# Down projection of six feed-forward blocks in seven products of quarter blocks, and another estimate of the shared port

## The chip, the cores and the metric

The kernel runs on one core of a Trainium2 chip. The metric is device time in microseconds (us) of one execution; the profile is of one execution of the same program. Engines are named as in the profile: PE (TensorE), PEld (its weight loads), DVE (VectorE), ACT (ScalarE), POOL (GpSimd), SP (the queue that issues the loads).

## The reference, cut to what matters

One layer of a decoder trunk for a prompt group of 512 tokens and a sample group of 8 x 4 tokens, all in float32. After four mixers and a first LayerNorm comes the feed-forward part, to which the change belongs:

```python
D_MODEL = 2048
D_FF = 4 * D_MODEL
...
mix = jnp.concatenate([y_a, y_b, y_c, y_d], axis=-1) @ lp['w_out']
x = layer_norm(ALPHA * x + mix, lp['ln1_g'], lp['ln1_b'])
ff = jnp.square(jax.nn.relu(x @ lp['w_up'])) @ lp['w_down']
x = layer_norm(ALPHA * x + ff, lp['ln2_g'], lp['ln2_b'])
```

## The kernel before

Activations lie transposed: a tile has 128 features on the partitions and 544 tokens (512 prompt, 32 sample) on the free axis, worked in two halves of HN = 272. The profile's names A, B, C, E and F are such slots of one pool; during the feed-forward part the 16 tiles `z` of the residual sum are E and A0 to A14, and the normalised input `x1h`, `x1l` lies in B, C and F.

Every float32 product is made of three matmuls in the rounded type fp32r: a value is split into a rounded part and the rest (`uh` and `ul`, `x1h` and `x1l`, for weights `wh` and `wl`), and `mm3` adds wh x xh, wh x xl and wl x xh. Weights come in parts of 128 x 1024 floats (512 KB) into a ring of `raw` buffers, loaded by SP (`emit_dma`); three of these buffers and four of each split ring exist from the start, and `widen` adds NRAW2 = 2 and NPIECE2 = 1 in the space that the mixers leave. A piece of 512 columns is split by one ACT copy into `wh` (`emit_split`) and one subtraction into `wl` (`emit_lo`), on DVE, or for units planned with None on DVE or POOL, whichever the planner's clocks say. Five pieces are made ahead of TensorE, and the next piece is begun when one has been used up (`piece_done`). A part's buffer is loaded anew after its last subtraction.

The feed-forward part goes over 8 blocks of 1024 hidden features. In each block 8 up tiles (16 k tiles x 2 halves x 3 = 96 matmuls of 272 columns each) are made, squared after relu and split (`up_done`); the first block's are made half by half as 16 units of 48 matmuls (`uph`). Then 16 down tiles (8 k tiles x 2 halves x 3 = 48 matmuls each) are added into `z` by DVE. Two down tiles share a unit of weights 256 columns wide. The last block's down tiles are made in two passes, with the second LayerNorm (`finish`) beside them. The first pass over `w_out` before the feed-forward part ends with units (`op`, `ob`) in which each accumulator takes a chain of 12 matmuls, 4 k tiles x 3, on one half.

The order of all instructions is fixed when the program is built, by a planner (`Model`): it keeps a clock for each engine, a price for each instruction, and for instructions of DVE and POOL the stretches in which they hold a port that the two share. Side work (`gens`) is put between matmuls when it is due by these clocks, and POOL or DVE is chosen by them. `in_sbuf` decides which inputs count as lying in SBUF. Tile names carry two numbers (such as acc_57_205), so that cutting off the last number leaves acc_57, which is not in the list ("s", "t", "o", "acc") of accumulators.

Every instruction is recorded at line 159, the planner's wrapper, so rows are told apart by tile names.

Of the kernel before, what the change touches and what calls it, by code (L numbers as in the profile page):

```python
# [33 lines left out]
NT = NP + NS  # L34
# [13 lines left out]
LN2_B = -2.12194440054690583e-4  # L48
SCALE = 0.125
NQ = 3  # L50
NRAW2, NPIECE2 = 2, 1
AT2, AT3 = 4.0, 4.0
NSTEP = 1
ZB, ZV = 0.0, 0.3
# [2 lines left out]
LV, LA, LM = 2.5, 2.0, 2.5  # L57
AHEAD = 3
GBIAS = 2.0


TABLES = {str(f) for f in (AF.Exp, AF.Sigmoid, AF.Sin, AF.Gelu_apprx_tanh, AF.Sqrt)}
# [80 lines left out]
class Engine:  # L143
    PER = {"V": (0.00104, 0.155), "A": (0.00083, 0.19), "G": (0.0021, 0.19)}

    @staticmethod
    def in_sbuf(x):

        name = getattr(x, "tensor", x).name
        return name.rsplit("_", 1)[0] not in ("s", "t", "o", "acc") and x.shape[-1] > 1  # L150

    def __init__(self, mdl, eng, name):
        self.mdl, self.eng, self.nme = mdl, eng, name
# [58 lines left out]
def tile_hybrid_trunk(ctx: ExitStack, tc: tile.TileContext, x_prompt, x_sample, cache_nsa_kv, cache_win_kv,  # L212
# [130 lines left out]

    NPIECE, NRAW, PART = 4, 3, 1024
    raws, pieces, parts, plan, split, pending = {}, [], [], [], {}, []
    st = {"piece": 0, "dma": 0}

    def add_unit(src, kc, cols, lo=None):

        i = len(plan)  # L350
        plan.append((kc, cols, lo))
        n = max(1, PART // cols)
        for a in range(0, kc, n):
            parts.append((i, src(a, min(a + n, kc)), min(n, kc - a), cols))
            w = min(n, kc - a) * cols
            for q in range(0, w, 512):
                pieces.append((i, a * cols + q, min(512, w - q), len(parts) - 1, q))
        return i

    def ring(tag, i, shape, dt, n, n2):  # L360

        if "wide" in st and (i - st["wide"][tag]) % (n + n2) < n2:
            return alloc(ffp, tag + "2", shape, dt, n2)
        return alloc(wgt, tag, shape, dt, n)
# [19 lines left out]
    def emit_split():  # L384

        pi = st["piece"]
        if pi >= len(pieces):
            return
        emit_lo()
        u, a, n, part, q = pieces[pi]  # L390
        hi = ring("wh", pi, (128, 512), F32R, NPIECE, NPIECE2)
        A.copy(hi[:, :n], raws[part][:, q:q + n])
        pending.append((pi, hi))
        st["piece"] = pi + 1

    def emit_lo():
        if pending:
            pi, hi = pending.pop()
            u, a, n, part, q = pieces[pi]
            raw = raws[part][:, q:q + n]  # L400
            lo = ring("wl", pi, (128, 512), F32R, NPIECE, NPIECE2)
            eng = plan[u][2]
            if eng is None:
                eng = V if mdl.clk["V"] + 0.65 + GBIAS < mdl.clk["G"] + 1.25 else G
            eng.tensor_sub(lo[:, :n], raw, hi[:, :n])
            split[u, a] = (hi, lo)
            if pi + 1 == len(pieces) or pieces[pi + 1][3] != part:
                if st["dma"] < len(parts):
                    emit_dma()
# [120 lines left out]
    def up_cols(b_, i):  # L530
        return lambda a, b: [(whole, dram2(w_up, a * 128 * DFF + b_ * 1024 + i * 128,
                                           [[DFF, 128], [128 * DFF, b - a], [1, 128]]))]

    def dn_cols(b_, n):
        return lambda a, b: [(whole, dram2(w_down, (b_ * 1024 + a * 128) * DM + n * 128,
                                           [[DM, 128], [128 * DM, b - a], [1, 256]]))]

    for h in range(2):
        for i in range(NA):
# [1 line left out]
    for b in range(NBLK):  # L541
        for i in range(NA if b == 0 else 0, 8):
            U["up", b, i] = add_unit(up_cols(b, i), KT, 128, V)
        for h in range(2 if b == NBLK - 1 else 1):
            for n in range(0, 16, 2):
                U["dn", b, h, n] = add_unit(dn_cols(b, n), 8, 256, None if b == NBLK - 1 else V)
# [1301 lines left out]

    x1h, x1l = mh, ml
    sums = {}  # L1850

    def lnq(h, tag, bufs=1):
        return alloc(S["lnp", h], "ln" + tag, (128, HN), F32, bufs)

    def sum_add(k, h):

        if k == 0:
            if not sums:
                sums["t"] = slot(lo_slots.pop())
            sums[h] = sums["t"][:, hs_(h)]  # L1860
            G.tensor_copy(sums[h], z[k][:, hs_(h)])
        else:
            G.tensor_add(sums[h], sums[h], z[k][:, hs_(h)])

    def norm_stats(ln, h):
# [3 lines left out]
        hold(mean)  # L1869
        mm(mean[:, :HN], ones_f, sums[h])  # L1870
        if "v" not in sums:
            sums["v"] = slot(lo_slots.pop())
        va, vb = sums["v"][:, :HN], sums["v"][:, HN:]
        yield mean,
        q = {}
# [82 lines left out]
    uh, ul = {}, {}  # L1958
    ur = lambda k: (uh[k], ul[k])

    def up_done(i, acc, hv=(0, 1)):
        if 0 in hv:
            uh[i], ul[i] = fq(f"uh{i}", F32R), fq(f"ul{i}", F32R)
        t = fq("sq", bufs=2)
        a, b = hv[0] * HN, hv[-1] * HN + HN
        tv = halves(t)[:, hv[0]:hv[-1] + 1]
        av = acc[:, hv[0]:hv[-1] + 1, :HN]
        A.activation(tv, av, AF.Relu)
        V.tensor_mul(tv, tv, av)
        split_hl(uh[i][:, a:b], ul[i][:, a:b], t[:, a:b])  # L1970

    for h in range(2):
        drain_side(("rstd", 1, h))
# [25 lines left out]
    def finish(h):  # L1999
# [6 lines left out]
        def chunk(c, i):  # L2006
# [10 lines left out]
            yield y,  # L2017
            V.tensor_scalar(nm_[:n, i, c:c + 1], s_[:n, i, c:c + 1], -1.0 / 512, None, op0=OP.mult)
            yield nm_,
            sq = fq("sq", bufs=2)  # L2020
            A.activation(sq[:n, :512], y[:n], AF.Square, bias=nm_[:n, i, c:c + 1], accum_out=m2[:n, i, c:c + 1])
            mdl.put(mdl.ready, m2, mdl.when(sq, read=False))
            flags.add(("st", h, c, i))
# [41 lines left out]
        for c in range(4):  # L2065
            for i in range(ng):
                yield rstd, ("lag", "V", 2.5)
                apply(c, i, nmu, rstd, t_)

    for b in range(NBLK):  # L2070
        for i in range(NA if b == 0 else 0, 8):
            up_done(i, run_tile(U["up", b, i], 0, 128, x1r, ks16, True))
        last = b == NBLK - 1
        if last:
            load_gb()
        for h in range(2 if last else 1):
# [43 lines left out]
```

## Time and profile before

| | |
|---|---|
| median of 3 runs | 2548.75 us (2545.38 to 2549.04) |
| profiled execution: its time, its span | 2549.48 us, 2547.7 us |
| mean granted clock of TensorE | 0.966 |
| busy: PE, PEld, DVE, ACT, POOL | 95%, 91%, 44%, 35%, 23% |
| DMA | 260.80 MB, 102 GB/s |

PE's busy share counts pipelined matmuls and says only that something was under way. What one matmul costs is read from the distance between the starts of neighbours.

### The profile page before, as it was taken

How to read it: one execution, taken by the hardware profiler on the slowest of the kernel's cores; microseconds unless marked ns; L12 is line 12 of the kernel's file. 1: busy time of each engine (PE TensorE's matmuls, PEld its weight loads, DVE VectorE, ACT ScalarE, POOL GpSimd, SP SyncE). 2: the span in 40 equal slices, each digit the busy share in tenths (PEclk: the TensorE clock that was granted, in tenths of full speed). 3: DMA queues.
4: the chain of work that ended last, by engine and by line, in shares of the span. 5: the costliest groups of instructions: out<-in, count | busy, mean ns of one | idle time of the engine just before them, and what ended most of it. 6: DMA issues, size and time to landing. Idle time of an engine off the chain costs nothing.

```text
span 2547.7 us, 46688 instructions
## 1 busy us (share of the span) xinstructions
PE 2417.4 (95%) x19283; PEld 2329.7 (91%) x19283; DVE 1112.8 (44%) x2009; ACT 882.5 (35%) x1725; POOL 594.1 (23%) x552
## 2 busy tenths in 40 slices
PE   6999999998998687999999999999999999999995
PEld 6999888988888486999999999999999999999995
DVE  6773344566645656333333333333333333333346
ACT  4443345554444445422222222222222212212353
POOL 2332235446446487400000000000000000000155
PEclk8999999999999787999999999999999999999998
DMA  7333322321386443423223223223223223223343
GB/s 222 72 84 83 117 71 61 88 76 52 94 216 207 116 125 108 141 90 94 83 86 98 84 84 99 84 83 96 88 83 93 91 84 91 92 84 92 124 152 110
DMA packets 378593, 260.80 MB, mean 102 GB/s; under 512 B 30143, under 2 KB 359963, under 8 KB 378308
## 3 DMA queue, kind: packets, MB, share of 16 engines
q1 hardware_dynamic: 377931, 256.88, 34.5%
q8 instruction: 151, 2.47, 0.4%
q0 software_dynamic: 448, 0.93, 0.2%
q14 instruction: 63, 0.51, 0.1%
HBM read 249.26 MB, written 12.85 MB: 103 GB/s over the span
## 4 chain that ended last, share of the span: by engine, by line
PE 80%; DVE 5%; DMA 2%; ACT 1%; issue 1%; POOL 1%; SPq 0%; POOLq 0%; ACTq 0%; DVEq 0%
PE acc L159 74%; PE s L159 3%; PE o L159 2%; PE t L159 1%; DVE C L159 1%; DVE A L159 1%; DMA page<-in_cache_nsa_kv_dram 1%; POOL wl L159 1%; DVE B L159 0%; DMA page<-in_cache_win_kv_dram 0%; POOL A L159 0%; DVE cp L159 0%; ACT kt L159 0%; DMA raw<-in_w_out_dram 0%; DVE c L159 0%
## 5 line engine op out<-in xcount | busy, mean ns | idle before, releaser
L159 PE MATMUL acc<-B,wh 128*128 128x272 f32 (+1 forms) x3552 | 984.4, 292 | 15.4 <-ACT B L159 6.1
L159 ACT CAST wh<-raw 128x512 fp32r<-128x512 f32 x797 | 491.9, 619 | 1246.5 <-PE acc L159 1199.9
L159 POOL TENSOR_TENSOR wl<-raw,wh 128x512 fp32r<-128x512 f32 x287 | 384.8, 1348 | 1685.5 <-ACT wh L159 1609.7
L159 PEld LDWEIGHTS acc<-B,wh 128*128 128x128 f32 (+1 forms) x3552 | 680.0, 191 | 23.5 <-ACT B L159 8.8
L159 PE MATMUL acc<-C,wh 128*128 128x272 f32 x2456 | 679.0, 293 | 10.2 <-DVE C L159 5.7
L159 DVE TENSOR_TENSOR wl<-raw,wh 128x512 fp32r<-128x512 f32 x510 | 364.0, 721 | 536.7 <-ACT wh L159 534.9
L159 PE MATMUL acc<-B,wl 128*128 128x272 f32 x2560 | 583.2, 293 | 1.8 <-POOL wl L159 1.8
L159 PE MATMUL acc<-uh,wh 128*128 128x272 f32 (+2 forms) x2048 | 559.1, 288 | 1.6 <-DVE A L159 1.6
L159 PE MATMUL acc<-ul,wh 128*128 128x272 f32 (+2 forms) x2048 | 554.0, 286 | 0.3 <-DVE fv L159 0.3
L159 PEld LDWEIGHTS acc<-C,wh 128*128 128x128 f32 x2456 | 468.7, 192 | 17.1 <-DVE C L159 11.6
L159 PE MATMUL acc<-uh,wl 128*128 128x272 f32 (+2 forms) x2048 | 444.5, 289 | 6.5 <-POOL wl L159 6.3
L159 PEld LDWEIGHTS acc<-B,wl 128*128 128x128 f32 x2560 | 425.5, 191 | 8.9 <-issue 5.2
L159 PEld LDWEIGHTS acc<-ul,wh 128*128 128x128 f32 x2048 | 387.9, 189 | 0.6 <-DVE fv L159 0.6
L159 PEld LDWEIGHTS acc<-uh,wh 128*128 128x128 f32 x2048 | 385.2, 188 | 1.8 <-ACT wh L159 1.7
L159 PEld LDWEIGHTS acc<-uh,wl 128*128 128x128 f32 x2048 | 325.1, 188 | 8.4 <-POOL wl L159 7.9
L159 PE MATMUL acc<-A,wh 128*128 128x272 f32 (+1 forms) x992 | 280.1, 300 | 0.0
L159 PE MATMUL acc<-A,wl 128*128 128x272 f32 (+1 forms) x992 | 215.6, 299 | 0.8 <-DVE wl L159 0.8
L159 DVE TENSOR_TENSOR A<-A,acc 128x544 f32<-128x544 f32 (+3 forms) x165 | 97.1, 589 | 261.3 <-PE acc L159 261.2
L159 PEld LDWEIGHTS acc<-A,wh 128*128 128x128 f32 (+1 forms) x992 | 189.4, 191 | 4.9 <-issue 2.1
L159 PEld LDWEIGHTS acc<-A,wl 128*128 128x128 f32 (+1 forms) x992 | 156.2, 189 | 10.9 <-issue 6.5
L159 DVE TENSOR_TENSOR sq<-sq,acc 128x544 f32<-128x544 f32 (+1 forms) x72 | 47.4, 658 | 197.8 <-ACT sq L159 197.8
L159 POOL TENSOR_TENSOR pl<-p,ph 128x512 fp32r<-128x512 f32 (+1 forms) x64 | 57.8, 902 | 77.2 <-ACT ph L159 66.9
(484 smaller groups left out, 1944.3 us busy)
## 6 DMA issues: line engine op xcount, KB each, us to landing
raw<-in_w_up_dram SPq DMA_DIRECT2D x144, 512.0 KB
raw<-in_w_down_dram SPq DMA_DIRECT2D x144, 512.0 KB
raw<-in_w_in_dram SPq DMA_DIRECT2D x52, 512.0 KB
page<-in_cache_nsa_kv_dram SPq DMA_DIRECT2D x64, 256.0 KB
raw<-in_w_out_dram SPq DMA_DIRECT2D x23, 512.0 KB
raw<-in_w_out_dram SPq DMA_DIRECT2D x34, 256.0 KB
C<-in_x_prompt_dram SPq DMA_DIRECT2D x16, 256.0 KB
raw<-in_w_in_dram SPq DMA_DIRECT2D x16, 256.0 KB
```

The costliest lines, as they stand in the source:

```text
L159: r = f(*a, **k)
```

## The change

In blocks 1 to 6 (`SEVEN`) the down projection is computed by Strassen's method in the form with seven products. The 2 x 2 blocks are: two neighbouring output tiles (n, n + 1), two neighbouring k tiles, and the two token halves. Numbered as in the code, the weight operands are, with W(k, n) a tile of `w_down`: 1: W(0,0); 2: W(1,0); 3: W(1,1); 5: W(0,1) - W(0,0); 6: W(1,1) - (5); 7: W(1,1) - W(0,1); 4: W(1,0) - (6). Operands 5, 6, 7 and 4 are four subtractions of 512 columns for each pair of output tiles (`combine`), on POOL or DVE as the planner's clocks say (TBIAS = 2.0 in favour of POOL). The activation operands are made in `up_done` for each pair of up tiles: four subtractions or additions of 272 columns, and splits of seven half tiles in place of four. For each pair of output tiles (a unit m, 8 of them) `seven` makes the products in the order 1, 5, 6, 2, 3, 7, 4, each a chain of 4 k pairs x 3 = 12 matmuls into an accumulator of its own, and DVE adds each product into the halves of `z` that it belongs to (eight adds of one half, and for 7 one add on both halves). During these blocks `z` is kept in another basis, which needs fewer additions; `basis` changes 16 half tiles on entering and again on leaving, as side work in the up stage. In the first unit the products 5, 6, 2 and 3 take the last k pair after the others.

A unit's weights come as two parts 128 columns wide in place of two 256 wide, and both buffers are loaded anew after the split of operand 3. NRAW2 goes from 2 to 1. The two `sq` buffers give way to one double `S` and to two slots that the first LayerNorm has left (`spare`), in `finish` too. `in_sbuf` now takes the name up to the first underscore, so that accumulators no longer count as SBUF inputs anywhere in the program: in the planner's estimate a DVE instruction on an accumulator and one tile no longer holds the shared port, and copies out of an accumulator are priced at the full rate.

```diff
--- before.py
+++ after.py
@@ -48,7 +48,7 @@
 LN2_B = -2.12194440054690583e-4
 SCALE = 0.125
 NQ = 3
-NRAW2, NPIECE2 = 2, 1
+NRAW2, NPIECE2 = 1, 1
 AT2, AT3 = 4.0, 4.0
 NSTEP = 1
 ZB, ZV = 0.0, 0.3
@@ -57,6 +57,7 @@
 LV, LA, LM = 2.5, 2.0, 2.5
 AHEAD = 3
 GBIAS = 2.0
+TBIAS = 2.0
 
 
 TABLES = {str(f) for f in (AF.Exp, AF.Sigmoid, AF.Sin, AF.Gelu_apprx_tanh, AF.Sqrt)}
@@ -147,7 +148,7 @@
     def in_sbuf(x):
 
         name = getattr(x, "tensor", x).name
-        return name.rsplit("_", 1)[0] not in ("s", "t", "o", "acc") and x.shape[-1] > 1
+        return name.split("_")[0] not in ("s", "t", "o", "acc") and x.shape[-1] > 1
 
     def __init__(self, mdl, eng, name):
         self.mdl, self.eng, self.nme = mdl, eng, name
@@ -343,6 +344,7 @@
 
     NPIECE, NRAW, PART = 4, 3, 1024
     raws, pieces, parts, plan, split, pending = {}, [], [], [], {}, []
+    quads, combos = {}, {}
     st = {"piece": 0, "dma": 0}
 
     def add_unit(src, kc, cols, lo=None):
@@ -357,6 +359,43 @@
                 pieces.append((i, a * cols + q, min(512, w - q), len(parts) - 1, q))
         return i
 
+    QUAD = (1, 5, 6, 2, 3, 7, 4)
+    def add_quads(srcs):
+        us_ = []
+        for two in srcs:
+            us_.append(len(plan))
+            plan.append((8, 128, V))
+            for src in two:
+                parts.append((us_[-1], src(0, 8), 8, 128))
+            quads[us_[-1]] = (len(parts) - 2, len(parts) - 1)
+            pieces.extend((us_[-1], p, 512, ("q", us_[-1]), 0) for p in QUAD)
+        return us_
+    def quad(u, k, n):
+        return raws[quads[u][n]].rearrange("p (q a c) -> p q a c", a=2, c=128)[:, :, k]
+    def q4(t):
+        return t.rearrange("p (q c) -> p q c", q=4)
+    def combine(u, k):
+        if (u, k) in combos:
+            return
+        t = combos[u, k] = q4(alloc(ffp, f"tt{k}", (128, 512), F32, 1))
+        a, b = {5: lambda: (quad(u, 0, 1), quad(u, 0, 0)), 6: lambda: (quad(u, 1, 1), combos[u, 5]),
+                7: lambda: (quad(u, 1, 1), quad(u, 0, 1)), 4: lambda: (quad(u, 1, 0), combos[u, 6])}[k]()
+        (V if mdl.clk["V"] + 0.7 + TBIAS < mdl.clk["G"] + 1.27 else G).tensor_sub(t, a, b)
+    def quad_src(u, k):
+        if k in (1, 2, 3):
+            return quad(u, *{1: (0, 0), 2: (1, 0), 3: (1, 1)}[k])
+        return combos[u, k]
     def ring(tag, i, shape, dt, n, n2):
 
         if "wide" in st and (i - st["wide"][tag]) % (n + n2) < n2:
@@ -388,8 +427,13 @@
             return
         emit_lo()
         u, a, n, part, q = pieces[pi]
+        if pi + 2 < len(pieces) and pieces[pi + 2][0] in quads and pieces[pi + 2][1] in (5, 6, 7, 4):
+            combine(*pieces[pi + 2][:2])
         hi = ring("wh", pi, (128, 512), F32R, NPIECE, NPIECE2)
-        A.copy(hi[:, :n], raws[part][:, q:q + n])
+        if u in quads:
+            A.copy(q4(hi), quad_src(u, a))
+        else:
+            A.copy(hi[:, :n], raws[part][:, q:q + n])
         pending.append((pi, hi))
         st["piece"] = pi + 1
 
@@ -397,8 +441,15 @@
         if pending:
             pi, hi = pending.pop()
             u, a, n, part, q = pieces[pi]
+            lo = ring("wl", pi, (128, 512), F32R, NPIECE, NPIECE2)
+            if u in quads:
+                V.tensor_sub(q4(lo), quad_src(u, a), q4(hi))
+                split[u, a] = (hi, lo)
+                for _ in range(2 if a == 3 else 0):
+                    if st["dma"] < len(parts):
+                        emit_dma()
+                return
             raw = raws[part][:, q:q + n]
-            lo = ring("wl", pi, (128, 512), F32R, NPIECE, NPIECE2)
             eng = plan[u][2]
             if eng is None:
                 eng = V if mdl.clk["V"] + 0.65 + GBIAS < mdl.clk["G"] + 1.25 else G
@@ -531,9 +582,11 @@
         return lambda a, b: [(whole, dram2(w_up, a * 128 * DFF + b_ * 1024 + i * 128,
                                            [[DFF, 128], [128 * DFF, b - a], [1, 128]]))]
 
-    def dn_cols(b_, n):
+    def dn_cols(b_, n, m=256):
         return lambda a, b: [(whole, dram2(w_down, (b_ * 1024 + a * 128) * DM + n * 128,
-                                           [[DM, 128], [128 * DM, b - a], [1, 256]]))]
+                                           [[DM, 128], [128 * DM, b - a], [1, m]]))]
+    SEVEN = range(1, NBLK - 1)
 
     for h in range(2):
         for i in range(NA):
@@ -541,6 +594,9 @@
     for b in range(NBLK):
         for i in range(NA if b == 0 else 0, 8):
             U["up", b, i] = add_unit(up_cols(b, i), KT, 128, V)
+        if b in SEVEN:
+            U["dq", b] = add_quads([[dn_cols(b, n + e, 128) for e in range(2)] for n in range(0, 16, 2)])
+            continue
         for h in range(2 if b == NBLK - 1 else 1):
             for n in range(0, 16, 2):
                 U["dn", b, h, n] = add_unit(dn_cols(b, n), 8, 256, None if b == NBLK - 1 else V)
@@ -1848,6 +1904,7 @@
 
     x1h, x1l = mh, ml
     sums = {}
+    spare = []
 
     def lnq(h, tag, bufs=1):
         return alloc(S["lnp", h], "ln" + tag, (128, HN), F32, bufs)
@@ -1856,7 +1913,8 @@
 
         if k == 0:
             if not sums:
-                sums["t"] = slot(lo_slots.pop())
+                spare.append(lo_slots.pop())
+                sums["t"] = slot(spare[-1])
             sums[h] = sums["t"][:, hs_(h)]
             G.tensor_copy(sums[h], z[k][:, hs_(h)])
         else:
@@ -1869,7 +1927,8 @@
         hold(mean)
         mm(mean[:, :HN], ones_f, sums[h])
         if "v" not in sums:
-            sums["v"] = slot(lo_slots.pop())
+            spare.append(lo_slots.pop())
+            sums["v"] = slot(spare[-1])
         va, vb = sums["v"][:, :HN], sums["v"][:, HN:]
         yield mean,
         q = {}
@@ -1958,16 +2017,50 @@
     uh, ul = {}, {}
     ur = lambda k: (uh[k], ul[k])
 
-    def up_done(i, acc, hv=(0, 1)):
+    ops = {}
+    def up_done(i, acc, hv=(0, 1), blk=0):
         if 0 in hv:
-            uh[i], ul[i] = fq(f"uh{i}", F32R), fq(f"ul{i}", F32R)
-        t = fq("sq", bufs=2)
+            for d, n in ((uh, "uh"), (ul, "ul")):
+                d[i] = fq(f"{n}{i}", F32R)
+        if blk:
+            t = slot(spare[i % 2])
+        else:
+            if i % 2 == 0:
+                S["S"] = fq("S", n=2 * NT)
+            t = S["S"][:, i % 2 * NT:(i % 2 + 1) * NT]
         a, b = hv[0] * HN, hv[-1] * HN + HN
         tv = halves(t)[:, hv[0]:hv[-1] + 1]
         av = acc[:, hv[0]:hv[-1] + 1, :HN]
         A.activation(tv, av, AF.Relu)
         V.tensor_mul(tv, tv, av)
-        split_hl(uh[i][:, a:b], ul[i][:, a:b], t[:, a:b])
+        if blk not in SEVEN:
+            split_hl(uh[i][:, a:b], ul[i][:, a:b], t[:, a:b])
+            return
+        k = i // 2
+        tv, h_, l_ = halves(t), halves(uh[i]), halves(ul[i])
+        if i % 2 == 0:
+            s_ = S["S"] = fq("S", n=2 * NT).rearrange("p (a n) -> p a n", a=4)
+            split_hl(h_[:, 0], l_[:, 0], tv[:, 0])
+            V.tensor_sub(s_[:, 3], tv[:, 0], tv[:, 1])
+            split_hl(h_[:, 1], l_[:, 1], s_[:, 3])
+            S["u1"] = tv
+            for j, p in ((0, 1), (1, 7)):
+                ops[p, k] = h_[:, j], l_[:, j]
+            return
+        u1, s_ = S["u1"], S["S"]
+        V.tensor_add(s_[:, 0], u1[:, 1], tv[:, 1])
+        V.tensor_sub(s_[:, 1], s_[:, 0], u1[:, 0])
+        g_ = [halves(fq(f"{n}s{k}", F32R)) for n in ("uh", "ul")]
+        split_hl(g_[0], g_[1], s_[:, 0:2])
+        V.tensor_sub(s_[:, 2], tv[:, 0], s_[:, 1])
+        split_hl(h_, l_, tv)
+        f_ = [fq(f"{n}f{k}", F32R, n=HN) for n in ("uh", "ul")]
+        split_hl(f_[0], f_[1], s_[:, 2])
+        for j, p, q in ((0, 5, 2), (1, 6, 4)):
+            ops[p, k], ops[q, k] = (g_[0][:, j], g_[1][:, j]), (h_[:, j], l_[:, j])
+        ops[3, k] = f_
 
     for h in range(2):
         drain_side(("rstd", 1, h))
@@ -2017,7 +2110,7 @@
             yield y,
             V.tensor_scalar(nm_[:n, i, c:c + 1], s_[:n, i, c:c + 1], -1.0 / 512, None, op0=OP.mult)
             yield nm_,
-            sq = fq("sq", bufs=2)
+            sq = slot(spare[i % 2])
             A.activation(sq[:n, :512], y[:n], AF.Square, bias=nm_[:n, i, c:c + 1], accum_out=m2[:n, i, c:c + 1])
             mdl.put(mdl.ready, m2, mdl.when(sq, read=False))
             flags.add(("st", h, c, i))
@@ -2067,10 +2160,67 @@
                 yield rstd, ("lag", "V", 2.5)
                 apply(c, i, nmu, rstd, t_)
 
+    def seven(us_):
+        acc = {}
+        def chain(p, m, ks):
+            u = us_[m]
+            if (u, p) not in split:
+                emit_lo()
+            hi, lo = split[u, p]
+            if 0 in ks:
+                acc[p] = new_acc()[:, 0] if p in (1, 2, 7) else psS() if p in (5, 3) else ps("t" if p == 6 else "o")
+            o_ = acc[p][:, :HN]
+            for k in ks:
+                xh_, xl_ = ops[p, k]
+                w = slice(k * 128, k * 128 + 128)
+                PE.matmul(o_, hi[:, w], xh_, start=k == 0, stop=False)
+                PE.matmul(o_, hi[:, w], xl_, start=False, stop=False)
+                step_side()
+                PE.matmul(o_, lo[:, w], xh_, start=False, stop=k == 3)
+                step_side()
+            if 3 in ks:
+                split.pop((u, p))
+                emit_split()
+                n = 2 * m
+                if p == 7:
+                    t = halves(z[n + 1])
+                    V.tensor_add(t, t, o_[:, None].to_broadcast([128, 2, HN]))
+                    return
+                for e, h in {1: ((0, 0), (1, 1)), 2: ((0, 0),), 5: ((0, 1), (1, 1)), 6: ((1, 1),), 3: ((1, 0),),
+                             4: ((0, 1),)}[p]:
+                    t = z[n + e][:, hs_(h)]
+                    V.tensor_tensor(t, t, o_, op=OP.subtract if p in (3, 4) else OP.add)
+        chain(1, 0, range(4))
+        for ks in ((0, 1, 2), (3,)):
+            for p in (5, 6, 2, 3):
+                chain(p, 0, ks)
+        for m in range(8):
+            for p in QUAD:
+                if m or p in (7, 4):
+                    chain(p, m, range(4))
+    def basis():
+        for m in range(8):
+            yield LAG_V,
+            t = z[2 * m + 1]
+            for o_ in (t[:, hs_(0)], z[2 * m][:, hs_(1)]):
+                V.tensor_sub(o_, t[:, hs_(1)], o_)
     for b in range(NBLK):
+        if b in (SEVEN[0], SEVEN[-1] + 1):
+            spawn(basis())
         for i in range(NA if b == 0 else 0, 8):
-            up_done(i, run_tile(U["up", b, i], 0, 128, x1r, ks16, True))
+            up_done(i, run_tile(U["up", b, i], 0, 128, x1r, ks16, True), blk=b)
         last = b == NBLK - 1
+        if b in SEVEN:
+            drain_side()
+            seven(U["dq", b])
+            continue
         if last:
             load_gb()
         for h in range(2 if last else 1):
```

## Rows read from the trace of the kernel before

**Rows 1.** Page: span and busy shares; forty slices with the granted clock.

```profile
span 2547.7 us, 46688 instructions
...
PE 2417.4 (95%) x19283; PEld 2329.7 (91%) x19283; DVE 1112.8 (44%) x2009; ACT 882.5 (35%) x1725; POOL 594.1 (23%) x552
...
PEclk8999999999999787999999999999999999999998
```

**Rows 2.** Chain that ended last, in time: start, length, what; around the feed-forward blocks.

```profile
1017.40 1.05 PE acc L159 x3
1018.46 1387.81 PE acc L159 x11091
2406.33 0.62 ACT wh L159
```

**Rows 3.** Stages: before them (first two), a down stage, an up stage.

```profile
core 0: us, PE busy (x) PEld busy (x) DVE busy (x) ACT busy (x) POOL busy (x), PEclk, DMA share, GB/s
...
900.00:1018.00 118.00, 96.50 (x624) 89.72 (x624) 68.33 (x112) 55.58 (x110) 96.10 (x86) 0.82 0.47 125
sum 1018.00, PE 919.03 PEld 835.46 DVE 569.70 ACT 449.51 POOL 482.74; mean PE 91.90 PEld 83.55 DVE 56.97 ACT 44.95 POOL 48.27
...
1355.00:1450.00 95.00, 95.00 (x760) 95.00 (x760) 30.86 (x46) 28.60 (x47) 0.00 (x0) 1.00 0.30 90
1261.00:1355.00 94.00, 94.00 (x757) 94.00 (x757) 33.67 (x49) 20.45 (x33) 0.00 (x0) 1.00 0.29 90
```

**Rows 4.** DVE in time: every second unit of a down stage; first and last of eight up tiles.

```profile
1105.10 0.72 DVE L159 SCALAR_TENSOR_TENSOR A<-A,acc 128x544 f32<-128x544 f32 x1 [4.65 <-PE acc L159]
...
1128.99 0.72 DVE L159 SCALAR_TENSOR_TENSOR A<-A,acc 128x544 f32<-128x544 f32 x1 [4.65 <-PE acc L159]
...
1171.83 0.72 DVE L159 TENSOR_TENSOR sq<-sq,acc 128x544 f32<-128x544 f32 x1 [2.83 <-ACT sq L159]
...
1256.15 0.72 DVE L159 TENSOR_TENSOR sq<-sq,acc 128x544 f32<-128x544 f32 x1 [2.82 <-ACT sq L159]
```

**Rows 5.** PE in time: 37 matmuls in `uph`, then 81 in `ob`, first and last.

```profile
1051.79 0.29 PE L159 MATMUL acc<-B,wh 128*128 128x272 f32 x1
...
1056.31 0.29 PE L159 MATMUL acc<-B,wh 128*128 128x272 f32 x1
...
915.74 0.29 PE L159 MATMUL acc<-B,wl 128*128 128x272 f32 x1
...
925.83 0.29 PE L159 MATMUL acc<-C,wh 128*128 128x272 f32 x1
```

**Rows 6.** Groups by shape, window 1261 to 1355 us: busy, mean ns of one, idle before.

```profile
L159 DVE TENSOR_TENSOR wl<-raw,wh 128x512 fp32r<-128x512 f32 x33 | 22.8, 691 | 24.4 <-ACT wh L159 24.4
L159 ACT CAST wh<-raw 128x512 fp32r<-128x512 f32 x33 | 20.4, 620 | 76.1 <-PE acc L159 76.1
L159 DVE TENSOR_TENSOR A<-A,acc 128x544 f32<-128x544 f32 x15 | 10.8, 721 | 35.7 <-PE acc L159 35.7
```

**Rows 7.** Groups by shape, window 300 to 880 us, where POOL works too.

```profile
L159 DVE TENSOR_TENSOR A<-A,acc 128x272 f32<-128x272 f32 x30 | 12.8, 429 | 10.6 <-PE acc L159 10.5
...
L159 POOL TENSOR_TENSOR wl<-raw,wh 128x512 fp32r<-128x512 f32 x119 | 160.4, 1354 | 104.6 <-ACT wh L159 86.9 <-PE acc L159 8.1 <-ACT kh L159 4.1
```

**Rows 8.** All engines in time: POOL and DVE subtractions that meet; two DVE ones in a row.

```profile
1022.96 2.53 POOL L159 TENSOR_TENSOR wl<-raw,wh 128x512 fp32r<-128x512 f32 x2
...
1024.69 1.36 DVE L159 TENSOR_TENSOR wl<-raw,wh 128x512 fp32r<-128x512 f32 x1 [2.53 <-ACT wh L159]
...
1173.90 1.29 DVE L159 TENSOR_TENSOR wl<-raw,wh 128x512 fp32r<-128x512 f32 x2
```

**Rows 9.** ACT and DVE in time: the work after an up tile.

```profile
1170.65 0.62 ACT L159 CAST wh<-raw 128x512 fp32r<-128x512 f32 x1 [2.38 <-PE acc L159]
1171.18 0.62 ACT L159 ACTIVATE sq<-acc 128x544 f32<-128x544 f32 x1
...
1172.58 0.65 ACT L159 CAST uh<-sq 128x544 fp32r<-128x544 f32 x1 [0.79 <-DVE sq L159]
1173.26 0.73 DVE L159 TENSOR_TENSOR ul<-sq,uh 128x544 fp32r<-128x544 f32 x1 [0.71 <-ACT uh L159]
```

**Rows 10.** Waits: SP's queue, window 1210 to 1600 us: total, times, longest.

```profile
SPq L159 <- DVE wl L159: 360.6, 65, 10.0
```

## The prediction

> **What bounds the kernel now.** I read the page first [rows 1]: PE is busy nearly throughout, and its granted clock shows a 9 (90% or more of full speed) in all slices but the first and a few others. That share alone proves nothing, so next comes the chain of waits [rows 2]: from 1018 to 2406 us it is one unbroken run of PE, 11,091 matmuls without a releaser. The stages [rows 3] say what stands beside it: in a down stage and in an up stage DVE works about a third of the time, ACT a quarter, POOL not at all, the clock is at its upper level (1.00, 2.4 GHz), and the DMA engines are 29 to 30% busy. So in blocks 1 to 6, where the change lies, only the number of matmuls counts, as long as the side engines keep up.
>
> The price of a matmul is the distance between starts. Two units of a down stage (192 matmuls) take 1128.99 - 1105.10 = 23.89 us, 0.1244 us each; seven up tiles (672) take 84.32 us, 0.1255 each [rows 4].
>
> **The change: matmuls.** A down stage falls from 16 x 48 = 768 matmuls to 8 x 7 x 12 = 672, of the same 272 columns. Before, it took 4 x 23.89 = 95.6 us. The new chains have 12 matmuls into one half, each with a new accumulator. Their like stand in the trace [rows 5]: in `uph`, three in a row into the same half cost 4.52/36 = 0.1256 us; in `ob`, chains of exactly 12 with a new accumulator each cost 10.09/80 = 0.1261, seams included. I take 0.1256: 84.4 us. The bounds are 83.6 (at 0.1244) and 84.7 (at 0.1261). The saving is 11.2 us a block (10.9 to 12.0), six times that is **67 us** (65 to 72).
>
> **DVE in the new down stage.** A unit of 84 matmuls takes 84 x 0.1256 = 10.55 us. In it DVE has seven splits of 0.69, eight adds of 0.43 and one of 0.72 [rows 6, 7]: 4.83 + 3.44 + 0.72 = 9.0 us, where an old unit of 11.94 us had 4 x 0.69 + 2 x 0.72 = 4.2. Durations overlap when instructions stand in a row: two splits end after 1.29, not 1.38 [rows 8], so 0.60 is the true spacing; with 0.09 less for each of 16 the sum is 7.6 us. ACT has 7 x 0.62 = 4.3 us. POOL has the four combinations, by its own row [rows 7] 4 x 1.35 = 5.4 us, if the planner puts them there. It will mostly, since POOL is otherwise idle and favoured; on DVE they would add 2.4 to 2.8 us, 10.0 to 11.8 in all.
>
> What DVE loses against POOL is the unknown. While POOL made two subtractions in a row (1022.96 to 1025.49), one on DVE took 1.36 us in place of 0.69 and ended 0.56 after POOL [rows 8]: it waited, +0.67. Bounds for the four combinations: nothing, and each one's whole 1.28 (two end after 2.53) with nothing of DVE's hidden under it, +5.1. The middle is nearer to the row. A combination needs only loaded weights and a free buffer, so POOL starts it early, and DVE's adds of products (one tile, one accumulator) can run beside it: adds of this form averaged 0.43 in the stage where POOL was busy. I take half a microsecond each, +2, so DVE needs 9.6 to 11 us of 10.55. That is close. But the splits are five pieces (5 x 12 x 0.1256 = 7.5 us) ahead at the start of each stage and the up stage refills them. A unit may therefore overrun by 0.9 us for all eight units before TensorE waits.
>
> The Trainium skill ("SBUF — State Buffer", section "Who interferes with whom") says that a DVE instruction with two SBUF inputs and a GpSimd instruction that reads SBUF take turns at one port, for the whole instruction, and that one with at most one SBUF input does not contend. By that the splits and combinations need 4 x 1.28 + 7 x 0.69 = 9.95 us of a unit, which fits, but with only 0.6 to spare. The two rows above agree with it. What it does if the order on DVE is bad is rival B.
>
> **The up stages.** For two up tiles (24.1 us) DVE gets four more half operations (0.43 each) and splits of 816 more columns (0.73 + 0.43), about 2.9 us beside the 8.4 of before (eight splits, two squares and two subtractions at 0.69, 0.72 and 0.73); ACT gets about 1.1. The basis change is 32 half operations in two blocks, 7 us in a 96 us stage each time. The cover is TensorE's 96 us; without it all this would cost about 3 us a pair. Cost: nothing.
>
> **The turn from up to down.** After the last up tile the second half of an operand pair is due. From rows [rows 9]: a split ahead on ACT 0.5, relu 0.65, square 0.75, two dependent half operations 0.8, ACT copy 0.67, DVE subtraction 0.73: 4.1 us until product 5 has its last k pair, about 4.9 until products 2 and 4 do, 5.7 until product 3 does. One waiting split on DVE adds 0.7. Products 1, 5, 6, 2 and 3 without their last pair cover 48 matmuls, 6.0 us, and product 3's last pair comes 1.1 later. Queued behind these on DVE are product 1's adds, which free an accumulator for product 7 at about 6.5; it starts at 7.5. Bounds: nothing, and 3 us if the adds and splits come in a bad order; I take 0.5 a block, **3 us**.
>
> **Loads.** Bytes are the same; a part has rows of 512 bytes in place of 1 KB. Up stages already load such rows, and their DMA share stands at 0.30 for 90 GB/s against 0.29 for 90 in the down stage [rows 3]. So nothing is lost there. One buffer of five is given up, half a unit's lead. SP waits for DVE to free buffers, 360.6/65 = 5.5 us a time [rows 10]: it is ahead. In the new stage the pair of loads for unit m + 2 is issued as TensorE starts unit m, and is first needed after unit m and two products of m + 1, 13.6 us later; 1 MB at 90/0.30 = 300 GB/s takes 3.5 us, an estimate. Cost: nothing; if the cover were gone, TensorE's five pieces still hide 7.5 us.
>
> **The planner.** The new port estimate alters the order everywhere, also in the first 1018 us, where PE is idle for 1018 - 919 = 99 us [rows 3], 21.5 of it from 900 to 1018, where LayerNorm is spread over POOL and DVE. It removes holds of the port that the 0.43 us rows do not bear out, but it also prices copies out of accumulators higher. I bound this at a tenth of the idle time, 10 us to either side, and take zero. The last stage keeps its work.
>
> **Sum.** 2549.5 (the profiled execution, 0.7 over the median) - 67 + 3 = **2485 us**. About 0.2%, 5 us, is what a measurement of this kernel can tell from no change.
>
> **Rivals.**
> A. DVE overruns a little: 12 us a unit against 10.55, from full durations (9.0) plus 3 us of waiting. Eight overruns of 1.45 less the 7.5 in store leave 4.1 us a block, 25 in all: 2510. For it: the sum of durations without overlap. Against it: an older unit's splits were spaced by ACT, not by DVE [rows 6], so DVE had no backlog.
> B. The slower side: DVE stands behind POOL for each whole combination, its adds queued behind the stopped split, and nothing overlaps: 9.0 + 5.1 = 14.1 us a unit. Eight overruns of 3.55 less 7.5 are 21 us a block, 125 in all: 2485 + 125 = 2610. It decides from 12.9 us a unit on (18.7 us over in eight units, 11.2 beyond the store, as much as the block saves). For it: POOL starts whenever its inputs are there, just ahead of a split too. Against it: the row shows 0.67 lost behind two POOL instructions, not 1.28 behind each. The Trainium skill's rule on the port, above, is this rival's if every order falls so; by it alone nothing says that they do.
> C. The turn is not covered: 3 to 5 us a block, 18 to 30 in all in place of 3: 2500 to 2512. For it: eight dependent steps. Against it: 6.0 us of cover for 4.1.
> D. No gain: seams between the short chains eat the 96 matmuls. 336 chains would have to cost 0.2 us more each. The 81 matmuls of `ob` span six such seams, and 0.1261 on the mean leaves no room for them. 2549.
>
> **Chances.** The forecast, 2470 to 2500, with the planner's 10 us within it: 0.68. A: 0.13. C: 0.11. B: 0.06. D: 0.02. A and C lie on the faster side, so faster 0.92, same 0.02, slower 0.06. The range reaches from 2472 (72 saved and some 5 from the planner) to 2516 (C, and A with it): it leaves out B, D and the edges.
>
> **What would show it.** Right: PE without a break in blocks 1 to 6, starts 0.125 to 0.126 us apart, a down stage of 84 to 86 us, DVE busy 75 to 95% of it and POOL about half. A would show as TensorE waiting for `wl` late in a down stage; C as one wait of some microseconds at the same place in each block, on the activation splits or an accumulator. B would show as DVE splits of 1.3 us and more in great number. The prediction would be wrong above all if products wait for accumulators that DVE frees late, or if the first 1018 us move by more than 10 us.

## Result and profile after

The changed kernel takes 2482.35 us (median of 4 runs, 2479.61 to 2486.67) against 2547.73: the ratio is 0.9746, 95% interval 0.9729 to 0.9763, some 65 us. The forecast was 2485. The total hides two errors that nearly cancel, so that it came out this close is luck in part.

The page of the kernel after, with the lines that answer to [rows 1]:

```profile
span 2477.5 us, 47026 instructions
...
PE 2343.9 (95%) x18707; PEld 2250.2 (91%) x18707; DVE 1515.8 (61%) x2704; ACT 994.0 (40%) x1941; POOL 842.7 (34%) x729
...
PEclk8999999999999988999999999999999999999998
```

There are 576 matmuls fewer, as counted, and DVE goes from 44% busy to 61%. To see where the time came from, take one landmark of each block, the square of its first up tile, here of blocks 1 and 7 of the kernel after (DVE in time):

```profile
1141.76 0.72 DVE L160 TENSOR_TENSOR C<-C,acc 128x544 f32<-128x544 f32 x1 [2.83 <-ACT C L160]
...
2250.89 0.72 DVE L160 TENSOR_TENSOR C<-C,acc 128x544 f32<-128x544 f32 x1 [2.83 <-ACT C L160]
```

Before, block 1's landmark stood at 1171.83 [rows 4]. So 30 us are gained before the first changed block. Six blocks take 1109.1 us, 184.9 each, where six old ones of 96.3 + 95.6 took 1151: 42 us are gained there, not 67 - 3. The two spans differ by 70 us (the profiled execution of the kernel after was the fastest of its four), so 2 us are lost in the tail.

An up stage still takes 96.3 us, so a down stage takes 184.86 - 96.31 = 88.55 us, 3.7 over the forecast 84.4 + 0.5. DVE in time, kernel after, with POOL, in the first down stage, the other engines left out (product 7's add on both halves, the one of 544 columns, marks each unit: 1239.14, 1250.15, 1261.15):

```profile
1237.38 1.29 POOL L160 TENSOR_TENSOR tt<-raw,raw 128x512 f32<-128x512 f32 x1 [1.58 <-DVE wl L160]
1237.57 1.65 DVE L160 TENSOR_TENSOR wl<-tt,wh 128x512 fp32r<-128x512 f32 x1
1239.14 0.71 DVE L160 TENSOR_TENSOR A<-A,acc 128x544 f32<-128x544 f32 x1
1239.37 1.30 POOL L160 TENSOR_TENSOR tt<-raw,tt 128x512 f32<-128x512 f32 x1 [0.69 <-DVE wl L160]
1239.78 1.43 DVE L160 TENSOR_TENSOR wl<-raw,wh 128x512 fp32r<-128x512 f32 x1
...
1242.08 0.77 DVE L160 TENSOR_TENSOR A<-A,acc 128x272 f32<-128x272 f32 x2
1242.78 0.68 DVE L160 TENSOR_TENSOR wl<-tt,wh 128x512 fp32r<-128x512 f32 x1
1243.38 0.77 DVE L160 TENSOR_TENSOR A<-A,s 128x272 f32<-128x272 f32 x2
1243.54 1.29 POOL L160 TENSOR_TENSOR tt<-raw 128x512 f32<-128x512 f32 x1 [2.88 <-DVE wl L160]
1244.08 1.30 DVE L160 TENSOR_TENSOR wl<-tt,wh 128x512 fp32r<-128x512 f32 x1
...
1245.52 1.29 POOL L160 TENSOR_TENSOR tt<-raw,tt 128x512 f32<-128x512 f32 x1 [0.69 <-DVE wl L160]
1245.65 1.72 DVE L160 TENSOR_TENSOR wl<-raw,wh 128x512 fp32r<-128x512 f32 x1
1247.29 0.42 DVE L160 TENSOR_TENSOR A<-A,acc 128x272 f32<-128x272 f32 x1
...
1250.15 0.71 DVE L160 TENSOR_TENSOR A<-A,acc 128x544 f32<-128x544 f32 x1
...
1261.15 0.71 DVE L160 TENSOR_TENSOR A<-A,acc 128x544 f32<-128x544 f32 x1
```

A unit takes 11.0 us. In each, four splits of 0.68 take 1.30 to 1.72: each ends some 0.55 after a combination on POOL ends. The four stops cost 0.62 + 0.75 + 0.97 + 1.04 = 3.4 us. Two of the four splits read `raw` and no combination, so they don't stand there for POOL's result. The two adds from an accumulator at 1243.38, beside a combination, are not stretched: 0.77 for two, as for the two at 1242.08 without POOL. All 192 combinations are on POOL. The stage view for six units shows DVE without an idle moment:

```profile
1239.10:1305.10 66.00, 64.46 (x506) 63.33 (x506) 66.00 (x99) 26.08 (x43) 29.68 (x23) 1.00 0.36 97
```

And what TensorE waits for in blocks 1 to 6 (engine and tile, releaser, total us, times, longest):

```profile
PE acc L160 <- DVE A L160: 8.6, 36, 0.3
PE s L160 <- DVE wl L160: 5.8, 6, 1.0
```

The first line is 6 waits a block for an accumulator, the second one wait of 1 us a block, at the turn. One of the first kind (PE in time):

```profile
1247.32 0.28 PE L160 MATMUL o<-uh,wl 128*128 128x272 f32 x1
1247.86 0.37 PE L160 MATMUL acc<-uh,wh 128*128 128x272 f32 x1 [0.26 <-DVE A L160]
1248.06 0.29 PE L160 MATMUL acc<-ul,wh 128*128 128x272 f32 x1
```

It is the first matmul of a unit. The accumulator that it takes is free with DVE's add of 1247.29, which stands in the queue behind the stopped split of 1245.65. By starts, such a wait costs 0.54 + 0.20 us in place of twice 0.125, so 0.49 us and not 0.26.

### The profile page after: what moved, and what is told of

Read it like the earlier page. It is cut to its first block, busy times and chain, and to the rows that moved or that the text cites. A ratio compares the mean times of both kernels' runs of the same rounds, so it can differ in the third digit from the quotient of the medians.

```text
span 2477.5 us, 47026 instructions
## 1 busy us (share of the span) xinstructions
PE 2343.9 (95%) x18707; PEld 2250.2 (91%) x18707; DVE 1515.8 (61%) x2704; ACT 994.0 (40%) x1941; POOL 842.7 (34%) x729
## 5 line engine op out<-in xcount | busy, mean ns | idle before, releaser
L160 PE MATMUL acc<-uh,wh 128*128 128x272 f32 (+2 forms) x1088 | 315.1, 294 | 12.8 <-DVE A L160 12.7
L160 PE MATMUL acc<-ul,wh 128*128 128x272 f32 (+2 forms) x1088 | 309.6, 289 | 0.3 <-DVE fv L160 0.3
L160 POOL TENSOR_TENSOR tt<-raw,raw 128x512 f32<-128x512 f32 x48 | 62.6, 1303 | 715.9 <-DMA raw<-in_w_down_dram 435.2
L160 PE MATMUL acc<-uh,wl 128*128 128x272 f32 (+2 forms) x1088 | 294.9, 290 | 5.7 <-POOL wl L160 5.7
L160 PEld LDWEIGHTS acc<-uh,wh 128*128 128x128 f32 x1088 | 206.3, 190 | 21.1 <-issue 16.6
L160 DVE TENSOR_TENSOR A<-A,acc 128x272 f32<-128x272 f32 (+3 forms) x283 | 139.1, 504 | 117.8 <-ACT A L160 79.1
L160 PEld LDWEIGHTS acc<-ul,wh 128*128 128x128 f32 x1088 | 206.7, 190 | 0.6 <-DVE fv L160 0.6
L160 PEld LDWEIGHTS acc<-uh,wl 128*128 128x128 f32 x1088 | 197.7, 190 | 7.0 <-POOL wl L160 6.9
L160 DVE TENSOR_TENSOR wl<-tt,wh 128x512 fp32r<-128x512 f32 x192 | 188.9, 984 | 8.4 <-ACT wh L160 8.4
L160 ACT CAST wh<-tt 128x512 fp32r<-128x512 f32 x192 | 118.6, 621 | 184.4 <-PE acc L160 103.2
```

Source lines behind the costliest of these rows:

```text
L160: r = f(*a, **k)
```

## Experiments

**The two halves apart.** First the planner's edit in the old kernel:

```diff
-        return name.rsplit("_", 1)[0] not in ("s", "t", "o", "acc") and x.shape[-1] > 1
+        return name.split("_")[0] not in ("s", "t", "o", "acc") and x.shape[-1] > 1
```

> The kernel before with one edit, the new estimate of the shared port in the planner. Theory 1: the 30 us by which block 1 starts earlier in the changed kernel come from the planner's new order alone, so this kernel takes about 2548 - 30 = 2518 us, with block 1's first squaring on DVE near 1142 us in place of 1172 and the same 191.9 us a block after it. Rival: the 30 us come from other parts of the change (one load buffer less, other scratch tiles), and this kernel takes 2543 to 2553 us.

Measured: 2524.66 us (2520.69 to 2526.59), ratio 0.9906, interval 0.9880 to 0.9933: 24 us. Block 1's landmark is at 1144.12, 27.7 us earlier than before, and the span is 25.8 us shorter (2521.9), so the 2 us lost in the tail are here too. Theory 1 holds, 6 us short of its number.

Then the rest of the change without it:

```diff
-        return name.split("_")[0] not in ("s", "t", "o", "acc") and x.shape[-1] > 1
+        cut = name.rsplit("_", 1)[0] if Engine.old else name.split("_")[0]
+        return cut not in ("s", "t", "o", "acc") and x.shape[-1] > 1
...
+        Engine.old = b < SEVEN[0]
```

> The changed kernel with the old port estimate up to the end of block 0 and the new one from block 1 on. Theory 1: only the gain of the six blocks stays, 42 us less 2 us lost in the tail, so 2508 us. Rival: the early gain belongs to the other edits, and the kernel stays at 2482 us.

Measured: 2505.66 us (2500.84 to 2508.77), ratio 0.9831 (0.9803 to 0.9859), 43 us. The two halves add up: 24 + 43 = 67 against 65 together. Block 1's landmark is at 1167.90, 3.9 us earlier than before, and the tail loses 2, so the other scratch tiles and the lost load buffer, which this kernel has too, leave over nothing that intervals as wide as 17 to 31 and 36 to 50 us could show.

**What sets the pace of the down stage.**

```diff
-        (V if mdl.clk["V"] + 0.7 + TBIAS < mdl.clk["G"] + 1.27 else G).tensor_sub(t, a, b)
+        V.tensor_sub(t, a, b)
```

> The changed kernel with all four combinations of a unit on DVE and none on POOL. Theory 1: in the down stage DVE is the bound (11.0 us a unit, of which 3.3 us are four subtractions stopped behind POOL); on DVE the combinations cost 4 x 0.60 = 2.4 us, DVE needs 7.6 + 2.4 = 10.0 us, TensorE's 10.55 us bound again: 0.45 us x 48 units less, about 2460 us. Rival: DVE's instructions don't overlap so far, 11.8 us a unit, 38 us more than now, about 2520 us.

Measured: 2466.93 us (2465.41 to 2468.26), ratio 0.9683 (0.9658 to 0.9707), 15 us less than the changed kernel's median. DVE in time, first down stage, the ends of three units:

```profile
1243.81 0.71 DVE L160 TENSOR_TENSOR A<-A,acc 128x544 f32<-128x544 f32 x1
...
1253.85 0.71 DVE L160 TENSOR_TENSOR A<-A,acc 128x544 f32<-128x544 f32 x1
...
1263.88 0.71 DVE L160 TENSOR_TENSOR A<-A,acc 128x544 f32<-128x544 f32 x1
```

DVE now does 20 instructions in 10.04 us, the sum of spacings to the hundredth (11 x 0.60 + 8 x 0.35 + 0.64), and catches up with TensorE through the stage. TensorE's waits for accumulators are gone; the one at the turn is left. The block period is 181.7 us (landmarks at 1147.26 and 2237.20), 3.2 less than in the changed kernel: 19 us over six blocks, where theory 1 worked out 22. Of that the median shows 15; this kernel's block 1 also starts 5.5 us later than in the changed kernel's profile. Up to there the five kernels that differ only in the down stages run the same work, and their landmarks lie between 1141.76 and 1147.26, so 5 us is what single executions differ by.

The control leaves the combinations out:

```diff
-        if (u, k) in combos:
-            return
+        return
...
     def quad_src(u, k):
-        if k in (1, 2, 3):
-            return quad(u, *{1: (0, 0), 2: (1, 0), 3: (1, 1)}[k])
-        return combos[u, k]
+        return quad(u, *{1: (0, 0), 2: (1, 0), 3: (1, 1), 5: (0, 1), 6: (1, 1), 7: (0, 1), 4: (1, 0)}[k])
```

> The changed kernel without the four combinations: operands 5, 6, 7 and 4 are loaded tiles instead of differences, so the down projection of six blocks is not the reference's; matmuls, splits and additions are as many as before. Theory 1: POOL's combinations stop DVE and set the pace; without them DVE needs 7.6 us a unit and TensorE sets it at 10.55, a down stage of 84 to 85 us in place of 88.5: about 2458 us. Rival: the 4 us a block over the forecast lie at the seams of the short chains or at the turn from up to down, and little changes: 2475 to 2482 us.

Measured: 2462.17 us (2458.14 to 2464.71), ratio 0.9657 (0.9631 to 0.9684). The block period is 181.65 us (1146.42 to 2236.32), the same as with the combinations on DVE. So on DVE they cost no time at all, and on POOL 3.2 us a block. A down stage takes 85.3 us; of the 0.9 over 84.4 the wait at the turn, still there, is enough, so the seams of the chains cost nothing that this can show.

In between:

```diff
-        (V if mdl.clk["V"] + 0.7 + TBIAS < mdl.clk["G"] + 1.27 else G).tensor_sub(t, a, b)
+        (V if k in (5, 7) else G).tensor_sub(t, a, b)
```

> The changed kernel with combinations 5 and 7 on DVE and 6 and 4 on POOL. Theory: a combination costs DVE's queue 0.83 us on POOL (as a stopped split) and 0.60 on DVE, so a unit needs 11.0 - 2 x 0.23 = 10.5 us, about TensorE's own 10.55: near the kernel with all four on DVE, 2465 to 2470. Rival: what stops DVE is any mixture of the two engines, and the unit stays near 11 us: 2478 to 2486.

Measured: 2472.22 us (2471.61 to 2475.65), ratio 0.9699 (0.9681 to 0.9718). A unit takes 10.62 us, close to the 10.5 worked out, but a block takes 183.3 (landmarks 1143.75 and 2243.53), 1.6 more than with four on DVE. The mechanism holds, the time was 2 us over its range: DVE, at 0.08 over TensorE's 10.54 a unit, never catches up with a backlog from the turn. In five of the six blocks TensorE waits some 0.76 us for an accumulator (3.8 in all), which the kernel with all four on DVE does not.

**The planner's gain.**

```diff
+        near = [x for x in wide if getattr(x, "tensor", x).name.split("_")[0] not in ("s", "t", "o", "acc")]
...
-        both = len(wide) > 1 and fn != "tensor_tensor_scan"
+        both = len(near) > 1 and fn != "tensor_tensor_scan"
```

(and `near` in the port's condition alike)

> The kernel before; in the planner only the holds of the port go by the new rule, copies out of accumulators keep their old price. Theory: the early gain (23 us in the planner's edit alone) comes from holds that the old estimate gave to DVE's instructions on accumulators, above all the 128 mask additions of prompt attention, so it comes whole: about 2524 us, prompt attention's last product with values near 644 us in place of 666. Rival: the price makes it, and this kernel stays at 2543 to 2552.

Measured: 2523.77 us, ratio 0.9908 (0.9877 to 0.9939), last product with values at 644.6: the whole gain.

The other half of the edit, the price of copies by the new rule and the port by the old:

```diff
+        near = [x for x in wide if getattr(x, "tensor", x).name.split("_")[0] not in ("s", "t", "o", "acc")]
...
-        fast = fn in ("tensor_copy", "tensor_scalar") and len(wide) == len(aps) - 1
+        hold = fn in ("tensor_copy", "tensor_scalar") and len(wide) == len(aps) - 1
+        fast = hold and len(near) == len(wide)
...
-        port = bool(wide) and fn != "memset" and (self.nme == "G" or self.nme == "V" and (both or fast))
+        port = bool(wide) and fn != "memset" and (self.nme == "G" or self.nme == "V" and (both or hold))
```

> The kernel before; in the planner only the price of DVE's copies out of accumulators is the new one, the holds of the port are the old. Theory: nothing, 2543 to 2552 us. Rival: the gain, 2524 us. A third: any new order moves the time by some 10 us either way.

Measured: 2549.89 us, ratio 0.9997 (0.9986 to 1.0009): nothing. As a control for chance:

```diff
-                c = max(n / 2250.0 + 0.004, 0.06)
+                c = max(n / 2245.0 + 0.004, 0.06)
```

> The kernel before with the planner's price of a matmul 0.2% higher (2245 in place of 2250 columns a microsecond), an edit that says nothing of the port. It asks what a mere change of order does. Theory: within 5 us of 2548. Rival, that any new order may gain or lose 20 us: 2525 or 2570.

Measured: 2548.77 us, ratio 1.0001 (0.9988 to 1.0014). This one other order moves nothing; the 24 us are not scatter of that sort.

Where in the program the holds matter was tried from both ends, with a switch at the end of prompt attention:

```diff
+        cut = name.split("_")[0] if Engine.new else name.rsplit("_", 1)[0]
...
     spawn(att_prompt())
+    Engine.new = True
...
         flags.add("attp")
+        Engine.new = False
```

> The kernel before, with the new rule only from the start of prompt attention to its end (in the planner's order), the old one ahead of it and after it. Theory: prompt attention is what the old estimate held up, so most of the gain is here: 2524 to 2530 us. Rival: the gain arises in the sample's attention and the first LayerNorm, and at most 5 us are gained: 2540 to 2550.

Measured: 2543.77 us, ratio 0.9989 (0.9974 to 1.0003): 3 us and not clear of zero, though the last product with values stands at 639.4 in place of 665.8. That theory fell. The profiled execution took 2537.27 us, 6.5 under the median, so its rows flatter this kernel. The complement:

```diff
     spawn(att_prompt())
...
         flags.add("attp")
+        Engine.new = True
```

> The kernel before, with the new rule only from the end of prompt attention on (the complement of the run with the rule in prompt attention alone, which gained 2 to 5 us though prompt attention ended 26 us earlier). Theory 1: what counts is the order of the sample's attention and the first LayerNorm, so this kernel shows most of the 23 us: 2525 to 2533. Theory 2: the two need each other (attention must end early and LayerNorm must use the room), so each alone gives little: 2540 to 2550.

Measured: 2533.05 us, ratio 0.9934 (0.9915 to 0.9952), 17 us; theory 1, at the end of its range. The stage view from 860 to 1040 us, the end of the sample's attention and the first LayerNorm (columns as in [rows 3]), for the kernel before, the rule in prompt attention alone, after it alone, and everywhere:

```profile
860.00:1040.00 180.00, 140.69 (x1001) 125.83 (x1001) 93.47 (x176) 81.05 (x162) 125.11 (x112) 0.76 0.39 106
```

```profile
860.00:1040.00 180.00, 143.65 (x1024) 131.92 (x1025) 97.65 (x179) 82.63 (x166) 132.39 (x116) 0.81 0.41 112
```

```profile
860.00:1040.00 180.00, 152.72 (x1116) 140.56 (x1117) 101.74 (x193) 88.12 (x177) 132.11 (x112) 0.80 0.43 117
```

```profile
860.00:1040.00 180.00, 156.66 (x1149) 146.19 (x1150) 105.75 (x191) 88.93 (x179) 132.34 (x110) 0.84 0.46 126
```

In the same 180 us TensorE does 1001, 1024, 1116 and 1149 matmuls. It is idle for 39.3, 36.4, 27.3 and 23.3 us of them, and its granted clock is 0.76, 0.81, 0.80 and 0.84: part of the gain is less waiting and part a faster clock, and the runs don't part the two. Two of its waits are for the end of the first LayerNorm, the last sum on POOL and then the first normalised tiles from ACT (waits from 600 to 1020 us, before, and the one that is left with the rule everywhere):

```profile
PE s L159 <- POOL A L159: 6.6, 1, 6.6
PE acc L159 <- ACT B L159: 6.1, 2, 5.8
```

```profile
PE acc L159 <- ACT B L159: 2.9, 2, 2.6
```

Waits for the tiles `C` that DVE makes there grow in return, from 3.4 to 9.6 us. The wait of 6.6 us is also gone with the rule after prompt attention alone, and stands as it was with the rule in prompt attention alone. The additions of LayerNorm's squares, before and with the rule everywhere (tile view: count, shortest/median/longest ns, first and last start):

```profile
L159 DVE TENSOR_TENSOR A<-A,lnsq x18: 441/857/1461, 821.1 to 992.5; 128x272 f32<-128x272 f32 x18
L159 POOL TENSOR_TENSOR A<-A,lnsq x10: 753/765/982, 821.5 to 991.8; 128x272 f32<-128x272 f32 x10
```

```profile
L159 DVE TENSOR_TENSOR A<-A,lnsq x23: 429/1177/1261, 832.5 to 956.3; 128x272 f32<-128x272 f32 x23
L159 POOL TENSOR_TENSOR A<-A,lnsq x5: 775/777/793, 832.2 to 924.5; 128x272 f32<-128x272 f32 x5
```

They end 36 us earlier, and 23 of 28 instead of 18 go to DVE.

**The turn, and a version that beats both.** In the kernel with all combinations on DVE, TensorE (PE) and DVE in time at the first turn:

```profile
1235.60 0.43 DVE L160 TENSOR_TENSOR ulf<-S,uhf 128x272 fp32r<-128x272 f32 x1
1235.95 0.69 DVE L160 TENSOR_TENSOR wl<-raw,wh 128x512 fp32r<-128x512 f32 x1
...
1236.69 0.39 PE L160 MATMUL s<-uhf,wl 128*128 128x272 f32 x1 [0.96 <-DVE wl L160]
```

The activation operands are in time; the split of weight 3 (`wl`) stands behind them in DVE's queue.

```diff
-            up_done(i, run_tile(U["up", b, i], 0, 128, x1r, ks16, True), blk=b)
+            acc = run_tile(U["up", b, i], 0, 128, x1r, ks16, True)
+            if b in SEVEN and i == 7:
+                emit_lo()
+            up_done(i, acc, blk=b)
```

> The kernel with all combinations on DVE, and in blocks 1 to 6 the subtraction for the piece of operand 3 put ahead of the work after the last up tile instead of behind it. In the trace TensorE waits 0.96 to 1.2 us once a block for that piece. Theory: this wait goes and nothing else is late, 6 x 1.0 = 6 us less than 2467, about 2461. Rival: the wait moves to the activation operands that are pushed back by 0.6 us: 2464 to 2467.

Measured: 2457.96 us (2454.78 to 2463.08), ratio 0.9639 (0.9615 to 0.9662), the fastest of all. The wait at the turn goes. TensorE's waits in blocks 1 to 6 shrink to one line, a new and shorter wait for an accumulator, so the rival has a small part in it:

```profile
PE acc L160 <- DVE E L160: 1.6, 6, 0.3
```

The block period is 180.9 us (1145.96 to 2231.51), 0.7 less; the medians differ by 9 us, of which the blocks explain 4.4. The spans of the two profiled executions differ by 5.0 (2463.9 and 2458.9). The other 4.6 of the medians no row explains; that they are scatter is likely, but not shown.

## Why the prediction was right, and where its steps failed

- **Matmuls: right.** 96 fewer a block, chains of 12 without seams: with DVE out of the way a down stage takes 181.66 - 96.31 = 85.35 us, and 180.93 - 96.31 = 84.62 with the turn mended, where 84.4 was forecast.
- **DVE against POOL: the mechanism right, the term too small.** I took half a microsecond for each combination and 9.6 to 11 us a unit; a combination stops a split by 0.62 to 1.04, 3.4 in all, and with the 7.6 from the spacings this makes the measured 11.0. The Trainium skill's rule ("SBUF — State Buffer", "Who interferes with whom") agrees with these rows: splits with two inputs in SBUF end behind POOL's instruction, adds of an accumulator beside it stay at 0.42.
- **The store of five pieces: the step that failed.** "A unit may therefore overrun by 0.9 us for all eight units before TensorE waits." The units overrun by 0.45, and TensorE waits in six of eight, not for weights but for accumulators (36 waits in six blocks): the adds stand in the same queue as the splits, so a DVE that is behind is behind with both, and the accumulators, six for seven products, are far fewer than a stage's worth. Rival A's overrun thus came at a third of its size: its 3 us of waiting are the measured 3.4, but the durations overlap as in the sum. It cost 3.2 us a block, near the 4.1 it was priced at, though not by its sign, a wait for `wl`. The sign of rival B, splits of 1.3 us and more in great number, is there too (25 of the 56 splits of a stage take more than 1.2 us), without its cost.
- **The turn: small as forecast, though twice the term, and the place wrong.** 1.0 us a block where I took 0.5; I had put the waiting split ahead of the operands, and it stands behind them.
- **The planner: the step that failed most.** "I bound this at a tenth of the idle time, 10 us to either side, and take zero." It gave 24 us (17 to 31). PE's idle time from 900 to 1018 us alone was 21.5, and I had named LayerNorm there as spread over POOL and DVE; the bound of a tenth came from no row. The gain comes from the holds of the port alone, in the planner's estimate, and mostly after prompt attention. Whether LayerNorm ends earlier because more additions go to DVE or because the side steps fall due earlier was not separated. The last stage, which I took to stay as it was, lost 2 us by the same edit.
- **Loads, up stages, ACT: right.** No wait for a load or for ACT's splits is among TensorE's waits in the six blocks.
- **The sum** came out because 24 us from the planner made up for some 20 lost on DVE and 3 at the turn. That the two are of a size is luck: both things that the prediction called above all signs of being wrong, waits for accumulators that DVE frees late and first 1018 us that move by more than 10, came true. Without the planner's half, 2505.66 was still in the wide range up to 2516, but above the 2470 to 2500 of the forecast.

## What to carry to other kernels

An engine whose queue both feeds TensorE and empties its accumulators has no store to live from: if its work a unit exceeds TensorE's, the loss begins almost at once (here in the second or third unit, at 0.45 us too much), so cost that queue by spacings plus stops, not by busy share. Giving work to a second engine that stops the first can cost more than doing it there: here 0.6 us on DVE against a stop of 0.85. And when an edit touches a planner's prices, price the stages with idle time in them one by one before calling the effect zero.

## What the runs showed of the hardware that I had not expected

POOL and DVE fell into step: a combination starts about 0.1 us after the end of the DVE split that releases it, and so ahead of the next split, so that each of POOL's 1.3 us instructions stopped one of DVE's (0.62 to 1.04 us), four times in each of the six units shown. The split that releases it is the one of the same operand in the unit before, since there is one buffer for each combination; whether a second buffer or another order on DVE would break the step was not tried. DVE's back-to-back spacing of 0.60 us for 512 columns, 0.35 for 272 and 0.64 for 544 held to the hundredth from unit to unit (10.04 us for 20 instructions).
